# A hybrid encoder layer: stores issued from ScalarE's queue, a convolution of 544 columns, a norm weight applied after the transpose

## The chip, the core and the metric

The kernel runs on one core of a Trainium2 chip. The metric is device microseconds of one launch. The core has TensorE (PE in the profile; its weight loads are PEld), VectorE (DVE), ScalarE (ACT), GpSimd (POOL) and SyncE (SP, which here only issues DMAs). ScalarE and GpSimd can issue DMAs as well; in the profile the part of an engine that issues is called ACTq, POOLq or SPq.

## What is computed

One layer of a streaming encoder, for 1024 new positions of one stream and 64 of another with a cache of 512 positions (T = 1088 columns):

```python
xn = _rmsnorm(x, p['norm_mix_w'])
proj = xn @ p['w_in']
z, xbc, dt_raw, q, k, v, gate_ssm, gate_att = jnp.split(proj, ...)

xbc_c, conv_new = _causal_dwconv(conv_past, xbc, p['ssm_conv_w'], p['ssm_conv_b'])   # width 4
xbc_c = jax.nn.silu(xbc_c)
...
y_ssm, ssm_new = _ssd_scan(xs, dt, a_neg, bm, cm, ssm_past, chunk_len)
y_ssm = _rmsnorm((y_ssm + D * xs) * jax.nn.silu(z), p['ssm_norm_w'])    # by group

q, k = rope(rmsnorm(q)), rope(rmsnorm(k))
o = _diff_attention(q, k_all, v_all, q_pos, k_pos, lam)                 # softmax 1 - lam * softmax 2
o = (_rmsnorm(o, p['subln_w']) * (1.0 - lambda_init)).reshape(b, t, ATT_V_WIDTH)

mix = sigmoid(gate_ssm) * (y_ssm @ p['w_branch_ssm']) + sigmoid(gate_att) * (o @ p['w_branch_attn'])
x = x + mix @ p['w_out']
h = _rmsnorm(x, p['norm_ffn_w']) @ p['w_up']
ha, hb = jnp.split(h, 2, axis=-1)
hc, ffn_new = _causal_dwconv(ffn_past, ha, p['ffn_conv_w'], p['ffn_conv_b'])
x = x + (jax.nn.silu(hc) * hb) @ p['w_down']
```

## The kernel before

Everything is float32. A large product is made of three matmuls on operands split in a high and a low half (`product`, lines 170 to 172: high by high, high by low, low by high). Activations lie transposed, features on partitions and the 1088 columns along the free axis, mostly in four quarters of 272 columns (`CH`).

The stages, with their place in the profiled execution:

- Input projections and the norms of q and k (0 to about 560 us).
- **Attention** (about 560 to 1120 us). `attend` works on one unit, a head and a block of up to 128 rows. Scores go to PSUM (`sc`, lines 1111 and 1112), VectorE takes the maximum (line 1116 or 1120), ScalarE the exponentials (1125), VectorE combines the two softmaxes (1129), PE transposes the result (`pt`, 1140), copies follow, and PE multiplies by the values (`po`, 1160). When a head's nine units are done, `head_out` forms its norm, scales the nine blocks of `o_t` (line 1178), transposes them, splits them in `oh` and `ol`, and stores both to `o_sc`.
- Attention alone would leave PE idle, so **filler** runs among it: `conv_tiles` and `gate_tiles` project the features of the scan and the gates, a quarter of 24 matmuls at a time, into two PSUM banks (`mm`). `conv_tiles` copies each quarter out into `pre` behind three columns of the quarter before (`tail`, copied by GpSimd, line 989), multiplies by the four taps (ScalarE line 999, VectorE three times line 1001), applies SiLU as tanh (ScalarE line 1002, VectorE line 1003), and stores to `x_sc`. `gate_tiles` stores to `g_sc`.
- **The scan** (about 1125 to 1500 us): 36 steps of `front` and `back`, chunk after chunk of 128 columns, four groups; each step loads `bc` with a broadcast from `a_sc`. `gated`, `normed` and `scaled` finish a span of up to 384 columns and store it to `y_sc`. Filler here is the first two branch products: `o` times its weights with the gate, stored to `m_sc`, and half of `y` times its weights, stored to `n_sc`. Side tiles (`b_g`, eight buffers) hold what is loaded beside them and what is stored.
- **The third branch product** (about 1505 to 1610 us) loads the gates (`g_sc`), `n_sc` and `m_sc` through the same side tiles; then output projection and feed-forward part to the end.

Order is not written by hand alone. The program is recorded in the order of the code, with rates that say how much filler goes between units (`ATT_STEPS`, `SCAN_STEPS`), and a scheduler that reckons with its own durations then orders each engine's instructions; `tc.high_priority` and `tc.issue_after` bind it in places. So a lighter instruction can move others. Each engine runs its own queue strictly in order, and a DMA that has to wait for its data holds all that stands behind it in its queue.

Before, every store named above is issued from SP, the queue that also issues nearly all loads (`load` is `nc.sync.dma_start`, `send` is `nc.scalar.dma_start`).

Of the kernel before, what the change touches and what calls it, by code (L numbers as in the profile page):

```python
# [9 lines left out]
F32 = mybir.dt.float32  # L10
R32 = mybir.dt.float32r
AF = mybir.ActivationFunctionType
# [5 lines left out]
P = 128  # L18
D = 1024
# [70 lines left out]
def hybrid_layer(ctx: ExitStack, tc: tile.TileContext, xT, xt, prm, cst, rope, wvd, win, wbs, wba, wout, wup, wdn,  # L90
# [149 lines left out]
                    out(m, c, to)  # L240
                    yield w

    def store(dst):
        return lambda m, c, t: load(out=dst[P * m : P * (m + 1), c : c + t.shape[1]], in_=t)

    def run(gen):
        for _ in gen:
# [729 lines left out]
    def conv_tiles(tiles):  # L977
        for f in tiles:
            tail = None

            def evac(ps, c, w):
                nonlocal tail
                n = min(w, TP - c)
                pre = cv_pool.tile([P, QW + 6], F32, name="pre", tag="pre", bufs=2)
                cc = cv_pool.tile([P, QW + 3], F32, name="cc", tag="cc", bufs=3)
                if tail is None:
                    G.memset(pre[:, 0:3], 0.0)
                else:
                    G.tensor_copy(pre[:, 0:3], tail)  # L989
                S.copy(pre[:, 3 : 3 + n], ps[:, :n])  # L990
                tail, m = pre[:, n : n + 3], w
                if n < w:
                    m = w + 3
                    G.tensor_copy(pre[:, n + 3 : n + 6], par[:, O_CS + 3 * f : O_CS + 3 * f + 3])
                    S.copy(pre[:, n + 6 : w + 6], ps[:, n:])
                    G.tensor_copy(conv_o[:, f, 0:3], tail)
                    G.tensor_copy(conv_o[:, f, 3:6], pre[:, w + 3 : w + 6])
                cw = lambda i: col(O_CW + 4 * f + i)
                act(cc[:, :m], pre[:, :m], AF.Identity, bias=col(O_CB + f), scale=cw(0))  # L999
                for i in range(1, 4):  # L1000
                    V.scalar_tensor_tensor(cc[:, :m], pre[:, i : i + m], cw(i), cc[:, :m], ALU.mult, ALU.add)  # L1001
                seen["tanh"] = act(pre[:, :m], cc[:, :m], AF.Tanh)
                V.scalar_tensor_tensor(cc[:, :m], pre[:, :m], 1.0, cc[:, :m], ALU.add, ALU.mult)  # L1003
                seen["stored"] = load(out=x_sc[P * f : P * (f + 1), c : c + n], in_=cc[:, :n])
                if n < w:
                    load(out=x_sc[P * f : P * (f + 1), c + n : c + w], in_=cc[:, n + 3 : m])

            yield from project(win[B_X + f], evac)

# [23 lines left out]
    with (tc.tile_pool(name="ak", bufs=1) as ak, tc.tile_pool(name="at", bufs=1) as at,  # L1033
          tc.tile_pool(name="psc", bufs=1, space=PSUM) as psc, tc.tile_pool(name="psa", bufs=1, space=PSUM) as pa):
        def head_tiles(h):
            def fetch(name, n, b, parts):
                t = ak.tile([P, n], R32, name=name, tag=name, bufs=b)
                for lo, src in parts:
                    load(out=t[lo : lo + src.shape[0]].bitcast(F32), in_=src)
                return t  # L1040

            by_head = lambda d: [d.rearrange("(x h) t -> h x t", h=16)[2 * h + c] for c in range(2)]
            q, k, ck = by_head(q_st), by_head(k_st), by_head(c_st)
            q_t, kh_t, kl_t, ch_t, cl_t = [[None] * 2 for _ in range(5)]
            sides = ((0, 512), (512, T))
            q_src = lambda c: [(0, q[0])] if c == 0 else [(0, q[1][64:128]), (64, q[1][0:64])]
            twice = lambda src, u: [(0, src[64 * u : 64 * u + 64]), (64, src[64 * u : 64 * u + 64])]

            def component(c, x):
                a, b = sides[x]  # L1050
                for to, name, parts in ((q_t, "q", q_src(c)), (kh_t, "kh", twice(k[c], 0)), (kl_t, "kl", twice(k[c], 1))):
                    to[c] = to[c] or [None] * 2
                    to[c][x] = fetch(f"{name}_{x}", b - a, 3, [(lo, src[:, a:b]) for lo, src in parts])

            def past(u, to, name):
                for c in range(2):
                    to[c] = fetch(name, PAST, 2, twice(ck[c], u))

            v_t = ak.tile([P, 9, P], F32, name="v_t", tag="v_t", bufs=2)
            cv_t = ak.tile([P, 4, P], F32, name="cv_t", tag="cv_t", bufs=2)  # L1060

            def values_of():
                load(out=v_t[:, :8], in_=v[0:TP, P * h : P * (h + 1)].rearrange("(a p) e -> p a e", p=P))
                load(out=v_t[:TS, 8], in_=v[TP:T, P * h : P * (h + 1)])

            def cached():
                past(0, ch_t, "ch_t")
                past(1, cl_t, "cl_t")
                load(out=cv_t, in_=cv[:, P * h : P * (h + 1)].rearrange("(a p) e -> p a e", p=P))

            if h == 0:
                for x in range(2):
                    for c in range(2):
                        component(c, x)
                values_of()
                later.append(cached)
            else:
                for x in range(2):
                    component(0, x)
                values_of()  # L1080
                for x in range(2):
                    component(1, x)
                cached()
            return q_t, kh_t, kl_t, ch_t, cl_t, v_t, cv_t

        def attend(h, i, tiles, o_t, ssq, s0):
# [78 lines left out]
        def head_out(h, o_t, ssq, s0):  # L1165
# [7 lines left out]
            V.tensor_tensor(out=ms, in0=ms, in1=t0, op=ALU.mult)  # L1173
            V.tensor_tensor(out=t1, in0=ms, in1=t0, op=ALU.mult)
            V.scalar_tensor_tensor(rs, t1, 1.5, t0, ALU.add, ALU.mult)
            for i in range(9):
                n = min(P, T - i * P)
                V.scalar_tensor_tensor(o_t[:n, i], o_t[:n, i], rs[:n, i : i + 1], wsub[:n], ALU.mult, ALU.mult)
            yield
            yield  # L1180
            for b0 in range(0, 9, 4):
                pt = pa.tile([P, 512], F32, name="pt2", tag="pt", bufs=2)
                top = min(9, b0 + 4)
                for i in range(b0, top):
                    n = min(P, T - i * P)
                    PE.transpose(pt[:, (i - b0) * P : (i - b0) * P + n], o_t[:n, i], ident[:n, :n])
                w = min(T, top * P) - b0 * P
                hi, lo = (at.tile([P, 512], R32, name=n, tag="a_t", bufs=AT)[:, :w] for n in ("oh", "ol"))
                S.copy(hi, pt[:, :w])
                V.tensor_tensor(out=lo, in0=pt[:, :w], in1=hi, op=ALU.subtract)  # L1190
                for u, t in enumerate((hi, lo)):
                    seen["out"] = load(out=o_sc[D * u + P * h : D * u + P * (h + 1), b0 * P : b0 * P + w], in_=t.bitcast(F32))
                yield

        fill(FIRST)
# [4 lines left out]
        lam = at.tile([P, 4], F32, name="lam")  # L1200
        lt = at.tile([P, 512], F32, name="lt", tag="a_t", bufs=AT)[:, :64]
        wsub = at.tile([P, P], F32, name="wsub")
        V.tensor_scalar_mul(wsub, par[:, O_SUB : O_SUB + P], 1.0 - LAMBDA_INIT)
# [23 lines left out]
        for h in range(8):  # L1227
# [25 lines left out]
    with (tc.tile_pool(name="sin", bufs=1) as sin, tc.tile_pool(name="sp", bufs=1) as sp,  # L1253
# [93 lines left out]
        def scaled(g, c, w, xs, zt, y, rs):  # L1347
# [11 lines left out]
                V.tensor_tensor(out=lo[:, js], in0=y[:, js], in1=hi[:, js], op=ALU.subtract)  # L1359
            for u, t in enumerate((zt, y)):  # L1360
                r0 = D * u + 4 * P * g
                load(out=y_sc[r0 : r0 + 4 * P, c : c + w].rearrange("(j p) t -> p j t", p=P), in_=t)

        ends = []

# [609 lines left out]
```

## Time and profile before

| what | value |
| --- | --- |
| median of three runs | 2420.58 us (2420.09 to 2423.67) |
| the profiled execution | 2425.83 us |
| its span, first to last instruction | 2424.0 us |
| granted TensorE clock | 0.997 |
| busy of the span: PE, PEld, DVE, ACT, POOL | 98%, 95%, 72%, 50%, 30% |
| matmuls | 18648 |

A busy PE is a PE with a matmul under way; the rows of a view give busy time, count and the mean of one instruction, and at the end how long the engine sat idle just before and what ended that. In the views in order of time the first two numbers are the start and the length in us, and a bracket gives the idle time before and its releaser.

### The profile page before, as it was taken

To read this page: it belongs to the slowest core of one execution; us is meant where nothing else is said; L and a number is where in the kernel's file an instruction comes from. 1 tells how busy PE (TensorE), PEld (TensorE's weight loads), DVE (VectorE), ACT (ScalarE), POOL (GpSimd) and SP (SyncE) were. 2 spreads that over 40 slices of the span, in tenths; PEclk is the share of its full clock that TensorE was granted. 3 is DMA by queue.
4 is the path that set the end of the run, shared out by engine and by line. 5 is a ranking of instruction groups with operands and counts; after the bars stand their busy time and mean duration, and the time that the engine had idled before them with its cause. 6 is when DMAs were issued, how large, how long until landed. Compare 5 with 4: busy or idle time off the path is not lost.

```text
span 2424.0 us, 49267 instructions
## 1 busy us (share of the span) xinstructions
PE 2379.3 (98%) x18648; PEld 2306.1 (95%) x18648; DVE 1750.6 (72%) x3150; ACT 1217.8 (50%) x2695; POOL 731.4 (30%) x773
## 2 busy tenths in 40 slices
PE   8999999999999999999999999999999999999998
PEld 8999999999999999999888899999999999999998
DVE  4678987646868778884789776656866767677765
ACT  6454454325656666665666564334543334352442
POOL 0032433321101101111444442012254455444444
PEclk9999999999999999999999999999999999999999
DMA  7773868536555544435978955764124424367976
GB/s 240 274 245 129 265 218 303 168 104 205 163 157 153 164 143 135 143 104 180 352 264 267 344 190 186 210 208 142 66 82 157 143 98 160 127 199 200 245 182 105
DMA packets 295087, 449.78 MB, mean 186 GB/s; under 512 B 36601, under 2 KB 188290, under 8 KB 294850
## 3 DMA queue, kind: packets, MB, share of 16 engines
q1 hardware_dynamic: 265506, 387.00, 49.5%
q0 software_dynamic: 11040, 26.34, 5.5%
q10 hardware_dynamic: 18304, 33.30, 3.7%
q8 instruction: 146, 2.39, 0.4%
q14 instruction: 91, 0.75, 0.1%
HBM read 294.03 MB, written 152.50 MB: 184 GB/s over the span
## 4 chain that ended last, share of the span: by engine, by line
PE 44%; DVE 6%; DMA 3%; issue 2%; ACT 1%; POOL 1%; SPq 0%; POOLq 0%; DVEq 0%; ACTq 0%
PE mx L1617 13%; PE mx L1791 6%; PE mm L1617 5%; PE mm L170 2%; PE mm L172 2%; PE mm L171 2%; PE mx L170 2%; PE mm L1791 2%; PE mx L172 2%; PE mx L171 2%; PE yi L1306 1%; PE stp L1318 1%; PE ye L1312 1%; DMA b<-y_sc 1%; DMA m_sc<-b_g 1%
## 5 line engine op out<-in xcount | busy, mean ns | idle before, releaser
L170 PE MATMUL mm<-b,w_hi 128*128 128x272 f32 x1376 | 408.7, 297 | 0.0
L172 PE MATMUL mm<-b,w_lo 128*128 128x272 f32 x1376 | 404.2, 294 | 0.0
L171 PE MATMUL mm<-b,w_hi 128*128 128x272 f32 x1376 | 403.0, 293 | 0.0
L170 PEld LDWEIGHTS mm<-b,w_hi 128*128 128x128 f32 x1376 | 259.5, 189 | 5.7 <-issue 3.4
L171 PEld LDWEIGHTS mm<-b,w_hi 128*128 128x128 f32 x1376 | 259.6, 189 | 4.5 <-issue 3.1
L172 PEld LDWEIGHTS mm<-b,w_lo 128*128 128x128 f32 x1376 | 259.1, 188 | 3.6 <-issue 2.5
L1617 PE MATMUL mx<-m,w_hi 128*128 128x272 f32 x792 | 152.3, 290 | 1.2 <-ACT m L419 1.2
L420 DVE TENSOR_TENSOR wh<-w_f,wh 128x512 fp32r<-128x512 f32 (+1 forms) x156 | 151.6, 973 | 0.7 <-ACT wh L419 0.7
L1001 DVE SCALAR_TENSOR_TENSOR cc<-pre,par,cc 128x272 f32<-128x272 f32 (+1 forms) x288 | 139.6, 488 | 9.8 <-ACT cc L999 7.5
L1617 PE MATMUL mx<-n,wh 128*128 128x272 f32 x1056 | 141.6, 288 | 1.1 <-DVE u L1644 1.1
L1125 ACT ACTIVATE p_t<-sc,mx 128x512 f32<-128x512 f32 (+6 forms) x144 | 106.2, 740 | 67.5 <-DVE mx L1116 37.4
L1617 PEld LDWEIGHTS mx<-n,wh 128*128 128x128 f32 x1056 | 135.7, 188 | 1.3 <-DVE u L1644 1.3
L989 POOL COPY pre<-pre 128x3 f32<-128x3 f32 x72 | 27.7, 385 | 346.3 <-DVE cc L1003 182.1
L563 POOL TENSOR_TENSOR ws<-w_f 128x512 f32<-128x512 f32 (+1 forms) x51 | 69.3, 1360 | 198.2 <-DMA w_f<-in_win_dram 82.0
L1617 PEld LDWEIGHTS mx<-m,w_hi 128*128 128x128 f32 x792 | 124.4, 188 | 1.4 <-ACT m L419 1.4
L170 PE MATMUL mx<-b,w_hi 128*128 128x272 f32 x416 | 122.9, 296 | 2.0 <-ACT w_hi L155 1.5
L172 PE MATMUL mx<-b,w_lo 128*128 128x272 f32 x416 | 121.5, 294 | 0.0
L171 PE MATMUL mx<-b,w_hi 128*128 128x272 f32 x416 | 121.4, 292 | 0.0
L1617 PE MATMUL mx<-m,w_lo 128*128 128x272 f32 x396 | 114.2, 289 | 0.0
L1626 ACT ACTIVATE cc<-pre,par 128x544 f32<-128x544 f32 (+1 forms) x44 | 37.2, 846 | 146.2 <-DVE pre L1661 145.3
L156 DVE TENSOR_TENSOR w_lo<-w_f,w_hi 128x1024 fp32r<-128x1024 f32 (+1 forms) x74 | 92.8, 1256 | 22.5 <-ACT w_hi L155 22.1
L419 ACT CAST wh<-w_f 128x512 fp32r<-128x512 f32 (+1 forms) x156 | 95.2, 613 | 27.0 <-POOL w_f L569 8.3
(463 smaller groups left out, 7311.7 us busy)
## 6 DMA issues: line engine op xcount, KB each, us to landing
w_f<-in_win_dram SPq DMA_DIRECT2D x40, 512.0 KB, 4.3
w_f<-in_wup_dram SPq DMA_DIRECT2D x80, 256.0 KB, 2.9
w_f<-in_win_dram SPq DMA_DIRECT2D x76, 256.0 KB, 3.3
bc<-a_sc SPq DMA_DIRECT2D x32, 512.0 KB, 7.1
b<-y_sc SPq DMA_DIRECT2D x24, 544.0 KB, 8.1
h_sc<-hb SPq DMA_DIRECT2D x44, 272.0 KB, 2.1
ht<-h_sc SPq DMA_DIRECT2D x22, 544.0 KB, 4.7
t_sc<-ht SPq DMA_DIRECT2D x22, 544.0 KB, 2.9
```

What stands on the lines that cost most here:

```text
L156: V.tensor_tensor(out=lo, in0=w, in1=hi, op=ALU.subtract)
L170: PE.matmul(ps, a_hi, b_hi, start=i == 0, stop=False)
L171: PE.matmul(ps, a_hi, b_lo, start=False, stop=False)
L172: PE.matmul(ps, a_lo, b_hi, start=False, stop=i == n - 1)
L419: S.copy(hi, src)
L420: V.tensor_tensor(out=lo, in0=src, in1=hi, op=ALU.subtract)
L563: G.tensor_tensor(out=s1, in0=q21, in1=q22, op=ALU.add)
L1001: V.scalar_tensor_tensor(cc[:, :m], pre[:, i : i + m], cw(i), cc[:, :m], ALU.mult, ALU.add)
L1125: act(p_t[:n, :nk], sc[c][:n, :nk], AF.Exp, bias=mx[:n, c : c + 1], accum_out=dst)
L1617: PE.matmul(ps, w[x][:, c], b[y][:, k], start=start and k == i == 0, stop=k == 3 and i == 2, skip_group_check=not start)
L1626: act(cc[:, :n], pre[h][:, :n], AF.Identity, bias=col(O_FB + f), scale=cw(0))
L1791: PE.matmul(ps, w[y][:, c], b[z][:, k], start=start and k == j == 0, stop=k == n - 1 and j == 2, skip_group_check=not start)
```

## The change

Four edits, in attention and the scan.

1. Stores of tiles that ScalarE wrote are issued by ScalarE (`send`): `g_sc` in `gate_tiles` (32 stores), the high halves of `o_sc` (24) and `y_sc` (6), and `n_sc` (32). Stores of tiles that VectorE wrote stay on SP, `m_sc` among them.
2. The convolution works on halves of 544 columns. Both quarters are copied into one `pre` tile of 550 columns, and the taps, tanh and store follow once for both. `cc` has two buffers instead of three.
3. In `head_out` the nine scalings by row factor and weight become one multiplication of eight blocks by the row factors, broadcast, and one of the ninth. The weight `wsub`, by column, becomes `wcol`, by partition, through one transpose on PE at the start of attention, and is applied in the two instructions that split the transposed head.
4. The cached keys and values of a head are loaded before its fourth unit instead of at its start, and `cv_t` has one buffer instead of two.

```diff
-    def store(dst):
-        return lambda m, c, t: load(out=dst[P * m : P * (m + 1), c : c + t.shape[1]], in_=t)
+    def store(dst, by):
+        return lambda m, c, t: by(out=dst[P * m : P * (m + 1), c : c + t.shape[1]], in_=t)
...
-                seen["stored"] = load(out=g_sc[P * j : P * (j + 1), c : c + w], in_=gt)
+                seen["stored"] = send(out=g_sc[P * j : P * (j + 1), c : c + w], in_=gt)
...
             def evac(ps, c, w):
-                nonlocal tail
+                nonlocal tail, pre
+                first = c % HT == 0
+                if first:
+                    pre = cv_pool.tile([P, HT + 6], F32, name="pre", tag="pre", bufs=2)
+                    if tail is None:
+                        G.memset(pre[:, 0:3], 0.0)
+                    else:
+                        G.tensor_copy(pre[:, 0:3], tail)
+                at = 3 + c % HT
                 n = min(w, TP - c)
-                pre = cv_pool.tile([P, QW + 6], F32, name="pre", tag="pre", bufs=2)
-                cc = cv_pool.tile([P, QW + 3], F32, name="cc", tag="cc", bufs=3)
...
-                S.copy(pre[:, 3 : 3 + n], ps[:, :n])
+                S.copy(pre[:, at : at + n], ps[:, :n])
                 if n < w:
...
+                if first:
+                    return
+                c -= QW
+                n, m = min(HT, TP - c), HT
+                tail = pre[:, n : n + 3]
...
+                cc = cv_pool.tile([P, HT + 3], F32, name="cc", tag="cc", bufs=2)
                 act(cc[:, :m], pre[:, :m], AF.Identity, bias=col(O_CB + f), scale=cw(0))
...
-            cv_t = ak.tile([P, 4, P], F32, name="cv_t", tag="cv_t", bufs=2)
+            cv_t = ak.tile([P, 4, P], F32, name="cv_t", tag="cv_t")
...
-            for i in range(9):
-                n = min(P, T - i * P)
-                V.scalar_tensor_tensor(o_t[:n, i], o_t[:n, i], rs[:n, i : i + 1], wsub[:n], ALU.mult, ALU.mult)
+            V.tensor_tensor(out=o_t[:, :8], in0=o_t[:, :8], in1=rs[:, :8].unsqueeze(2).to_broadcast([P, 8, P]), op=ALU.mult)
+            V.tensor_scalar(o_t[:TS, 8], o_t[:TS, 8], rs[:TS, 8:9], None, ALU.mult)
...
-                S.copy(hi, pt[:, :w])
-                V.tensor_tensor(out=lo, in0=pt[:, :w], in1=hi, op=ALU.subtract)
+                act(hi, pt[:, :w], AF.Copy, scale=wcol)
+                V.scalar_tensor_tensor(lo, pt[:, :w], wcol, hi, ALU.mult, ALU.subtract)
                 for u, t in enumerate((hi, lo)):
-                    seen["out"] = load(out=o_sc[...], in_=t.bitcast(F32))
+                    seen["out"] = (send, load)[u](out=o_sc[...], in_=t.bitcast(F32))
...
+        pw = pa.tile([P, 512], F32, name="pw", tag="pt", bufs=2)
+        PE.transpose(pw[:, :P], wsub, ident)
+        S.copy(wcol, pw[:, 0:1])
...
+                if x == 3 and later:
+                    later.pop()()
...
-                load(out=y_sc[r0 : r0 + 4 * P, c : c + w].rearrange("(j p) t -> p j t", p=P), in_=t)
+                (send, load)[u](out=y_sc[r0 : r0 + 4 * P, c : c + w].rearrange("(j p) t -> p j t", p=P), in_=t)
...
-            yield from branch(True, side, o_sc, wba, D, (), store(m_sc))
-            yield from branch(True, side, y_sc[: 2 * D], wbs[0], None, (), store(n_sc))
+            yield from branch(True, side, o_sc, wba, D, (), store(m_sc, load))
+            yield from branch(True, side, y_sc[: 2 * D], wbs[0], None, (), store(n_sc, send))
```

PE executes the same matmuls in both kernels, and one transpose more after the change. How the instructions move is shown at three places.

SP, from the last spans of the scan (`y_sc<-y`) to the first loads of the third branch product (line 200), before:

```order
L218 DMA b_19331<-y_sc 128x4x272
L244 DMA n_sc<-b_g 128x272
L1353 DMA y_sc<-y 128x4x320
L218 DMA b_19339<-y_sc 128x4x272
L244 DMA n_sc<-b_g 128x272
L154 DMA w_f<-in_wbs_dram 128x1024
L218 DMA b_19341<-y_sc 128x4x272
L218 DMA b_19351<-y_sc 128x4x272
L244 DMA n_sc<-b_g 128x272 x3
L200 DMA b_g<-g_sc 128x272
L200 DMA b_g<-n_sc 128x272
```

The same place after the change (line 1365 is the `y_sc` store):

```order
L218 DMA b_18799<-y_sc 128x4x272
L1365 DMA y_sc<-y 128x4x320
L218 DMA b_18807<-y_sc 128x4x272
L154 DMA w_f<-in_wbs_dram 128x1024
L218 DMA b_18809<-y_sc 128x4x272
L218 DMA b_18819<-y_sc 128x4x272
L200 DMA b_g<-g_sc 128x272
L200 DMA b_g<-n_sc 128x272
```

The five `n_sc` stores (line 244) are gone from here; they stand in ScalarE's queue, each behind the copy that fills its tile.

VectorE, at the start of head 2's second unit, the wide one of rows 896 to 1023 (`ors` are the row factors of head 1, `sc` and `mx` scores and maxima of head 2's units), before:

```order
L1115 MEMSET sc 64x64
L1003 SCALAR_TENSOR_TENSOR cc<-pre,cc 128x272
L1169 TENSOR_TENSOR ms<-ms,ssq 128x9
L1116 TENSOR_REDUCE mx<-sc 128x1
L1236 MEMSET ssq 128x9
L1172 TENSOR_SCALAR ms<-ms 128x9
L1173 TENSOR_TENSOR ms<-ms,on_9065 128x9
L1174 TENSOR_TENSOR on_9066<-ms,on_9065 128x9
L1175 SCALAR_TENSOR_TENSOR ors<-on_9066,on_9065 128x9
L1178 SCALAR_TENSOR_TENSOR o_t<-o_t,ors,wsub 128x128 x4
L1127 RECIPROCAL sm<-sm 128x1
L1178 SCALAR_TENSOR_TENSOR o_t<-o_t,ors,wsub 128x128 x4
```

After the change, where line 1136 is the combination of the unit's softmaxes and lines 1183 and 1184 are the scaling:

```order
L1135 SCALAR_TENSOR_TENSOR sm<-sm,nlam,s_8796 128x1
L1127 TENSOR_REDUCE mx<-sc 128x2
L1136 SCALAR_TENSOR_TENSOR p_t<-p_t,sm 128x1024
L1180 TENSOR_TENSOR ms<-ms,on_8921 128x9
L1009 SCALAR_TENSOR_TENSOR cc<-pre,par,cc 128x544
L1134 RECIPROCAL sm<-sm 128x1
L1181 TENSOR_TENSOR on_8922<-ms,on_8921 128x9
L1009 SCALAR_TENSOR_TENSOR cc<-pre,par,cc 128x544
L1135 SCALAR_TENSOR_TENSOR sm<-sm,nlam,s_8796 128x1
L1182 SCALAR_TENSOR_TENSOR ors<-on_8922,on_8921 128x9
L1183 TENSOR_TENSOR o_t<-o_t,ors 128x1024
L1184 TENSOR_SCALAR o_t<-o_t,ors 64x128
```

The scaling of the finished head has moved behind the wide unit's combination (`p_t` 128x1024); before, it stood ahead of it. On PE, between this unit's last score and its first transpose, stood 72 filler matmuls before and stand 54 after the change.

VectorE again, near the end of attention, where head 6's scaling meets the maxima of a wide unit of head 7, before:

```order
L1115 MEMSET sc 64x64
L1178 SCALAR_TENSOR_TENSOR o_t<-o_t,ors,wsub 128x128 x8
L1178 SCALAR_TENSOR_TENSOR o_t<-o_t,ors,wsub 64x128
L1001 SCALAR_TENSOR_TENSOR cc<-pre,par,cc 128x272
L1116 TENSOR_REDUCE mx<-sc 128x1
```

And after the change:

```order
L1183 TENSOR_TENSOR o_t<-o_t,ors 128x1024
L1184 TENSOR_SCALAR o_t<-o_t,ors 64x128
L1122 MEMSET sc 64x64
L1011 SCALAR_TENSOR_TENSOR cc<-pre,cc 128x544
L1122 MEMSET sc 64x64
L1123 TENSOR_REDUCE mx<-sc 128x1 x2
```

The scaling keeps its place ahead of the maxima; nine instructions have become two.

More of the change, by code (lines that the diff above doesn't have):

```diff
@@ L1004, in evac @@
                 seen["stored"] = load(out=x_sc[P * f : P * (f + 1), c : c + n], in_=cc[:, :n])
-                if n < w:
-                    load(out=x_sc[P * f : P * (f + 1), c + n : c + w], in_=cc[:, n + 3 : m])
+                if n < HT:
+                    load(out=x_sc[P * f : P * (f + 1), c + n : c + HT], in_=cc[:, n + 3 : m])
             yield from project(win[B_X + f], evac)
@@ L1082, in head_tiles @@
                     component(1, x)
-                cached()
+            later.append(cached)
             return q_t, kh_t, kl_t, ch_t, cl_t, v_t, cv_t
@@ L1188, in head_out @@
                 hi, lo = (at.tile([P, 512], R32, name=n, tag="a_t", bufs=AT)[:, :w] for n in ("oh", "ol"))
-                S.copy(hi, pt[:, :w])
-                V.tensor_tensor(out=lo, in0=pt[:, :w], in1=hi, op=ALU.subtract)
+                act(hi, pt[:, :w], AF.Copy, scale=wcol)
+                V.scalar_tensor_tensor(lo, pt[:, :w], wcol, hi, ALU.mult, ALU.subtract)
                 for u, t in enumerate((hi, lo)):
-                    seen["out"] = load(out=o_sc[D * u + P * h : D * u + P * (h + 1), b0 * P : b0 * P + w], in_=t.bitcast(F32))
+                    seen["out"] = (send, load)[u](out=o_sc[D * u + P * h : D * u + P * (h + 1), b0 * P : b0 * P + w], in_=t.bitcast(F32))
                 yield
@@ L1202, in hybrid_layer @@
         wsub = at.tile([P, P], F32, name="wsub")
+        wcol = at.tile([P, 1], F32, name="wcol")
         V.tensor_scalar_mul(wsub, par[:, O_SUB : O_SUB + P], 1.0 - LAMBDA_INIT)
+        pw = pa.tile([P, 512], F32, name="pw", tag="pt", bufs=2)
+        PE.transpose(pw[:, :P], wsub, ident)
+        S.copy(wcol, pw[:, 0:1])
         for i in range(2):
```

17 lines of the change are left out of this document (6 added, 11 removed).

## The prediction

> **What bounds the kernel now.** I read the page's head first, then the busy time by stretch, then the waits of TensorE alone. Only TensorE is nearly always busy, and the change touches two stretches: attention (540 to 1100 us) and the scan with the branch products (1100 to 1560).
>
> ```profile
> span 2424.0 us, 49267 instructions
> PE 2379.3 (98%) x18648; PEld 2306.1 (95%) x18648; DVE 1750.6 (72%) x3150; ACT 1217.8 (50%) x2695; POOL 731.4 (30%) x773
> ...
> 540.00:1100.00 560.00, 557.24 (x4274) 535.05 (x4274) 441.95 (x1062) 355.36 (x954) 67.39 (x164) 1.00 0.49 150
> 1100.00:1560.00 460.00, 449.60 (x3606) 410.09 (x3606) 337.35 (x464) 263.82 (x619) 163.56 (x108) 1.00 0.78 255
> ```
>
> The columns are length, then busy time with instruction counts for PE, PEld, DVE, ACT, POOL, then the granted clock, DMA share and GB/s. PE is idle for 560 - 557.24 = 2.76 us in attention and for 460 - 449.60 = 10.40 us after it. The clock is full. So 13.2 us is all that lighter side engines can give back: 0.5% of the time. What those microseconds wait for is in the view of waits, for PE from 540 to 1560 us:
>
> ```profile
> PE yi L1306 <- DVE y L1314: 3.1, 2, 1.6
> PE tr L1285 <- DVE xx L1294: 2.3, 3, 1.4
> PE mx L170 <- ACT w_hi L155: 1.5, 1, 1.5
> PE sc L1111 <- ACT p_t L1125: 1.1, 1, 1.1
> PE stp L1318 <- DVE state L1325: 1.0, 2, 0.8
> ...
> PE yi L1306 <- ACT y L1316: 0.7, 1, 0.7
> PE cb L1287 <- ACT b_cb L1290: 0.6, 1, 0.6
> ...
> PE gst L1340 <- POOL zin L1336: 0.5, 1, 0.5
> ```
>
> Total us, times and longest stand behind each. The six rows on yi, tr, stp, cb and gst are the scan's: 3.1 + 2.3 + 1.0 + 0.7 + 0.6 + 0.5 = 8.2 us. The row of sc is attention's, the row of w_hi belongs to the branch products behind the scan.
>
> **The wider convolution and the norm.** Their prices, before and in the nearest rows of the new shape:
>
> ```profile
> L1001 DVE SCALAR_TENSOR_TENSOR cc<-pre,par,cc 128x272 f32<-128x272 f32 (+1 forms) x288 | 139.6, 488 | 9.8 <-ACT cc L999 7.5
> L1003 DVE SCALAR_TENSOR_TENSOR cc<-pre,cc 128x272 f32<-128x272 f32 x94 | 40.6, 432 | 6.8 <-ACT pre L1002 6.5
> L1628 DVE SCALAR_TENSOR_TENSOR cc<-pre,par,cc x88: 773/786/1884, 1729.8 to 2188.9; 128x544 f32<-128x544 f32 x44, 128x546 f32<-128x546 f32 x44
> L1178 DVE SCALAR_TENSOR_TENSOR o_t<-o_t,ors,wsub x72: 332/343/373, 651.9 to 1126.2; 128x128 f32<-128x128 f32 x64, 64x128 f32<-64x128 f32 x8
> L156 DVE TENSOR_TENSOR w_lo<-w_f,w_hi 128x1024 fp32r<-128x1024 f32 x29 | 35.3, 1216 | 2.5 <-ACT w_hi L155 2.4
> ```
>
> VectorE's convolution falls from 288 x 0.488 + 96 x 0.432 = 182 us to 144 x 0.786 + 48 x 0.73 (an estimate: 0.786 less the 0.056 that separates the first two rows) = 148 us, so 34 us less. The norm's 72 x 0.343 = 24.7 us become 8 x (1.216 + at most 0.343) = 12.5 us, 12 us less. ScalarE's two passes and GpSimd's copies halve in number as well. None of these 46 us is on the path by itself: VectorE has 560 - 442 = 118 us idle in attention. They count where PE waits for VectorE, and that is one place, shown in order of time:
>
> ```profile
> 1061.41 2.47 DVE L1178 SCALAR_TENSOR_TENSOR o_t<-o_t,ors,wsub 128x128 f32<-128x128 f32 x9
> ...
> 1064.22 1.07 DVE L1116 TENSOR_REDUCE mx<-sc 128x1 f32<-128x896 f32 x1
> 1065.33 1.01 ACT L1125 ACTIVATE p_t<-sc,mx 128x896 f32<-128x896 f32 x1 [2.63 <-DVE mx L1116]
> 1066.48 0.39 PE L1111 MATMUL sc<-kh,q 128*128 128x256 f32 x1 [1.08 <-ACT p_t L1125]
> ```
>
> The nine scalings of a finished head (2.47 us) hold back the maximum, that holds back the exponential, and PE waits 1.08 us for the score banks. In the new order the scaling still stands ahead of these maxima, but takes about 1.2 + 0.3 us. That is 1.0 us sooner, less 0.2 to 0.3 because the convolution instruction between them grows from 0.43 to 0.73 us. Term: **-0.8 us** (bounds -1.1 and 0).
>
> The added transpose `pw` is one more instruction on PE ahead of the first scores. Its nearest row is the transposes of attention:
>
> ```profile
> L1140 PE MATMUL pt<-con,p_t x328: 221/272/331, 584.4 to 1116.6; 128*128 128x128 f32 x144, 64*128 64x64 f32 x16, 64*64 64x64 f32 x4
> ```
>
> Term: **+0.3 us** (0 to 0.6, if it also waits a little for `wsub`). Carrying `wcol` as a scale costs no instruction.
>
> **The tighter order.** The scheduler reckons with the lighter VectorE and brings transposes closer behind their scores. The tightest case is unit 7 of head 2. Its last score and the end of its softmax were:
>
> ```profile
> 714.06 0.39 PE L1112 MATMUL sc<-kl,q 128*128 128x512 f32 x1
> ...
> 724.68 1.27 DVE L1129 SCALAR_TENSOR_TENSOR p_t<-p_t,sm 128x1024 f32<-128x1024 f32 x1
> ...
> 1061.89 0.29 PE L172 MATMUL mm<-b,w_lo 128*128 128x272 f32 x1
> 1063.78 0.29 PE L172 MATMUL mm<-b,w_lo 128*128 128x272 f32 x1
> ```
>
> So 725.95 - 714.45 = 11.5 us of softmax. The last two rows give the pace of filler: 15 matmuls from one to the other, 0.126 us each. The new order leaves 54 filler matmuls and about 1.9 us of attention's own between the two, where 72 stood: 54 x 0.126 + 1.9 = 8.7 us. If the softmax stayed as long, PE would wait 11.5 - 8.7 = 2.8 us. But nine scalings (9 x 0.343 = 3.1 us) no longer stand inside it. Bounds 0 and +2.8; I take **+1.0 us**, nearer the lower one. The single `cv_t` buffer waits for nothing: its load is now issued at the fourth unit and read by the ninth.
>
> **Stores from ScalarE.** 32 of `g_sc`, 24 of `o_sc`, 6 of `y_sc` and 32 of `n_sc`, 94 in all, leave SP. What one costs ScalarE when work follows directly:
>
> ```profile
> 349.58 0.33 ACTq L681 DMA_DIRECT2D z_sc<-pre  x1
> 349.95 0.39 ACT L688 COPY u<-mx 128x272 f32<-128x272 f32 x1 [0.40 <-ACT pre L666]
> ```
>
> That is 0.33 to 0.40 us, 31 to 38 us over 94, on an engine idle for 205 us in attention and for 196 after it: nothing on the path where it is covered, and the rival below where it is not. What it gives shows at two places on SP. First, in the scan:
>
> ```profile
> 1273.36 0.37 SPq L1362 DMA_DIRECT2D y_sc<-zin  x1
> ...
> 1280.07 5.58 DMA m_sc<-b_g
> 1285.67 0.32 SPq L200
> 1286.04 3.92 DMA bc<-a_sc
> ...
> 1291.89 0.33 PE L1306 MATMUL yi<-bc,xx 128*64 128x128 f32 x2 [1.64 <-DVE y L1314]
> ```
>
> The middle rows are from the chain that ended last. A store of `m_sc` lands after 5.58 us, SP waits for it before it reuses a side tile, the load of `bc` stands behind that on SP, and PE waits 1.64 us soon after. The big `y_sc` store of the same queue was issued just ahead. With the six of them on the other queue I expect `m_sc` to land sooner, and half of the scan's 8.2 us to go: **-4.1 us** (bounds -8.2 and, since the order changes too, +1.6, one more wait like the longest of them). That half is a choice: the waits on yi, whose chain this is, are 3.8 of the 8.2.
>
> The Trainium skill's page "DMA: Bandwidth & Descriptors" (Issuing engines are not separate DMA queues) speaks against this: DMAs of all issuing engines share the same 16 DMA engines and interleave, and spreading them saves only issue time on the sequencer. By that the term would be nothing and the sum -1.0 us, the first rival below; the trace of before does not decide it.
>
> Second, where the scan ends and the third branch product begins:
>
> ```profile
> 1506.33 1.95 SPq L244 DMA_DIRECT2D n_sc<-b_g  x3
> 1508.33 0.62 SPq L200 DMA_DIRECT2D b_g<-g_sc  x1
> ...
> 1513.35 3.86 DMA b_g<-n_sc
> ...
> 1528.34 0.43 ACT L226 ACTIVATE b_g<-b_g 128x272 f32<-128x272 f32 x1 [0.89 <-DMA b_g<-n_sc]
> 1528.68 1.03 ACT L155 CAST w_hi<-w_f 128x1024 fp32r<-128x1024 f32 x1
> ```
>
> The third row is from the chain, the others from the timeline. Three `n_sc` stores take SP 1.95 us right ahead of the branch's first loads; the chain of those loads, the tanh and the casts runs until ScalarE reaches the weight cast at 1528.68, for which PE waits 1.5 us. The new order has no store there, so the loads can start 2 us sooner: **-1.5 us** (bounds -1.5 and 0).
>
> **The sum.** -0.8 + 0.3 + 1.0 - 4.1 - 1.5 = -5.1 us. The profiled execution took 2425.83 us, of which 2424.0 are span; it would take 2420.7. It is 5.2 us above the median of the runs, 2420.58, so the forecast for the median is 2415.5 us, 0.21% less.
>
> **Rivals.**
> - *The stores bring only issue time.* The scan's 8.2 us stay; the other terms hold: -0.8 + 0.3 + 1.0 - 1.5 = -1.0 us, 2419.6. For it: `m_sc` remains on SP, with the loads that VectorE needs behind it, and VectorE itself is busy 337 of 460 us there. Against it: the 5.58 us landing right behind a large store. Chance 0.37.
> - *ScalarE's stores hold up the banks* (slower). Each makes ScalarE wait for its own result before the next copy out of PSUM. In scan and branch 38 of them stand, between exponentials and copies on which PE depends; at 0.40 us that is 15.2 us. If half reaches PE: +7.6 - 1.0 = +6.6 us, 2427.2. It decides once 15 of the 38 delay PE, since 15 x 0.40 = 6.0 exceeds the gain of 1.0 and the bound of 4.8 together. Against it: ScalarE is idle 43% of that stretch, and has issued such stores all through the input stage. Chance 0.13.
> - *The order falls worse throughout*: waits of the kind of 2.8 us above at several units and in the scan, +5 us or more, about 2426. Chance 0.08.
>
> **How the numbers follow.** The forecast has the remaining chance, 0.42. A change within 0.2% (4.8 us) is about what a measurement of this kernel cannot tell from none; the three runs lie 3.6 us apart. Faster by more than that is the forecast, 0.42; the first rival lies within, 0.37; the other two are slower, 0.21. The range begins at 2409, where nearly all 13.2 us of idle time would be gone, and ends at 2428, just past the case in which half the stores reach PE.
>
> **What would show it.** Right: PE idle from 1100 to 1560 near 5 us instead of 10.40; no wait of PE on `w_hi` near 1528; none of 1 us on `p_t`; VectorE 46 us less busy; `bc` loads with shorter waits of SP on `m_sc`. Wrong: the same waits on yi and tr in the scan (first rival); new waits of PE on copies by ScalarE, with ScalarE idle behind its own stores (second); waits on `p_t` before transposes around unit 7 of head 2 (third).

## The result and the profile after

The changed kernel is slower: 2432.64 us median (2427.73 to 2435.62, six runs) against 2421.47 (2420.09 to 2424.81, six runs). The ratio is 1.0042, 95% interval 1.0028 to 1.0055. The forecast was 2415.5 us, and the range 2409 to 2428 misses the median by 4.6 us. The profiled execution of the changed kernel took 2427.73 us, the shortest of its runs, so this trace shows less than the whole loss: its span is only 2.0 us longer than before's.

The page's head and the busy time by stretch, after (columns as in the prediction):

```profile
span 2426.0 us, 48596 instructions
PE 2380.8 (98%) x18649; PEld 2308.7 (95%) x18649; DVE 1712.4 (71%) x2902; ACT 1202.7 (50%) x2600; POOL 704.6 (29%) x725
...
540.00:1100.00 560.00, 558.65 (x4295) 537.68 (x4295) 416.96 (x826) 339.73 (x864) 40.29 (x118) 1.00 0.48 150
1100.00:1560.00 460.00, 445.47 (x3536) 405.90 (x3535) 328.63 (x441) 261.98 (x610) 165.63 (x106) 0.99 0.77 253
```

VectorE is 38 us less busy. In attention PE's idle time fell from 2.76 to 1.35 us. From 1100 to 1560 us it rose from 10.40 to 14.53 us, and the granted clock, 1.00 before, is 0.99. The waits of PE in that stretch, after:

```profile
PE tr L1297 <- DVE xx L1306: 3.0, 2, 2.4
PE yi L1318 <- ACT y L1328: 2.5, 1, 2.5
PE cb L1299 <- ACT b_cb L1302: 1.8, 1, 1.8
PE yi L1318 <- DVE bc L1310: 1.4, 2, 1.2
PE gst L1352 <- POOL zin L1348: 1.4, 1, 1.4
PE yi L1318 <- DVE y L1326: 0.8, 2, 0.5
...
PE mx L170 <- ACT w_hi L155: 0.4, 1, 0.4
```

The lines stand 12 higher than before's (L1318 is L1306's matmul). The longest wait was 1.64 us before; now three are of 2.4 us, 2.5 us and 1.8 us, and two of them are on ScalarE. The row that the prediction wanted shorter, yi on VectorE's `y`, did fall, from 3.1 to 0.8 us; other rows took its place.

**The wait of 2.5 us** is told by the chain of waits from 1139 to 1152 us (start, us, what), and by ScalarE's row in order of time:

```profile
1140.93 7.37 DMA w_f<-in_wba_dram
...
1148.33 0.02 ACTq L973
...
1148.38 0.33 ACTq L973
1148.71 0.04 issue
1148.75 0.59 ACT y L1328
1149.34 0.04 issue
1149.39 1.09 PE yi L1318 x16
```

```profile
1145.30 2.45 ACT L1309 ACTIVATE bc<-bc,nacum 128x128 f32<-128x128 f32 x8
1148.38 0.33 ACTq L973 DMA_DIRECT2D g_sc<-gt  x1
1148.75 0.59 ACT L1328 COPY y<-yi 128x512 f32<-128x512 f32 x1 [1.00 <-DMA w_f<-in_wba_dram]
```

ACTq L973 is a store of `g_sc` from ScalarE's queue. It has nothing to do with the weights `w_f`, yet it waited until they had landed, and ScalarE's copy of `y` out of PSUM stood behind it, and PE behind that. By the trace's semaphore records SP's and ScalarE's transfers take eight semaphores in turn, and this store has the semaphore of the eighth transfer before it, that load. But ScalarE was busy with exponentials until 1147.75 us, so the store accounts for 1.0 us of the 2.5 (the bracket of the copy: 0.6 us for the landing, the rest for the issue). The rest is the exponentials ahead of it, 0.8 us, and the copy itself, 0.6 us. At 1366 us the same happens with an `n_sc` store. There ScalarE had been idle since 1363.3 us, and the whole wait of 1.8 us is the store's:

```profile
1357.54 8.96 DMA m_sc<-b_g
1366.50 0.02 issue
1366.52 0.02 ACTq L244
1366.54 0.04 issue
1366.58 0.34 ACTq L244
1366.92 0.04 issue
1366.96 0.38 ACT b_cb L1302
```

So these two stores account for 2.8 us of the 14.53 us of idle time.

**After some waits PE runs at half speed.** Five stretches of the changed kernel in the view of busy time, the granted clock third from the end; the first is the wait of 2.5 us itself, at full clock; the stretch from 1188 us stands behind two waits of 1.2 and 0.5 us:

```profile
1146.50:1149.30 2.80, 0.41 (x4) 0.18 (x2) 0.00 (x0) 1.80 (x7) 0.00 (x0) 1.00 1.08 354
1150.40:1153.80 3.40, 3.40 (x16) 3.24 (x15) 2.97 (x5) 2.19 (x8) 2.10 (x2) 0.50 1.04 370
1153.80:1158.00 4.20, 4.20 (x38) 3.37 (x37) 3.17 (x5) 1.43 (x6) 0.76 (x1) 1.00 1.08 386
1188.00:1194.80 6.80, 6.24 (x28) 5.32 (x27) 6.80 (x9) 3.70 (x11) 2.46 (x2) 0.50 1.00 345
1379.10:1382.50 3.40, 3.14 (x15) 3.04 (x16) 3.40 (x6) 1.64 (x7) 1.40 (x1) 0.50 0.49 187
```

PE was busy 3.40 + 6.24 + 3.14 us at half speed, which costs half of that, 6.4 us. Before has no such stretch in the scan. So the scan costs 4.1 us of idle time and 6.4 us of clock more, 10.5 together, and the rest of the span gives 8.5 back. Much of that is attention. These are the scores' and the products' rows of before, then of after; the first and last starts are what counts:

```profile
L1111 PE MATMUL sc<-kh,q x208: 191/341/500, 566.0 to 1095.7; 128*128 128x512 f32 x73, 128*128 128x384 f32 x8, 128*128 128x256 f32 x8, 128*64 128x64 f32 x8
L1160 PE MATMUL po<-v_t,a_t x592: 269/275/377, 589.0 to 1120.1; 128*128 128x128 f32 x192, 64*64 64x128 f32 x6
```

```profile
L1118 PE MATMUL sc<-kh,q x208: 191/341/497, 564.8 to 1091.5; 128*128 128x512 f32 x73, 128*128 128x384 f32 x8, 128*128 128x256 f32 x8, 128*64 128x64 f32 x8
L1167 PE MATMUL po<-v_t,a_t x592: 269/275/356, 587.0 to 1115.1; 128*128 128x128 f32 x192, 64*64 64x128 f32 x6
```

From the first score to the last product: 554.1 us before, 550.3 after. About 0.9 us of the 3.8 is filler that the new order puts into the scan.

### The profile page after: what moved, and what is told of

Its sections match the earlier page's. It is cut to its first block, busy times and chain, and to the rows that moved or that the text cites. A ratio compares the mean times of both kernels' runs of the same rounds, so it can differ in the third digit from the quotient of the medians.

```text
span 2426.0 us, 48596 instructions
## 1 busy us (share of the span) xinstructions
PE 2380.8 (98%) x18649; PEld 2308.7 (95%) x18649; DVE 1712.4 (71%) x2902; ACT 1202.7 (50%) x2600; POOL 704.6 (29%) x725
## 4 chain that ended last, share of the span: by engine, by line
PE 54%; DVE 5%; DMA 4%; issue 2%; ACT 1%; POOL 1%; SPq 0%; ACTq 0%; POOLq 0%; DVEq 0%
PE mx L1629 13%; PE mx L1803 6%; PE mm L1629 5%; PE mm L170 4%; PE mm L172 4%; PE mm L171 4%; PE mx L170 2%; PE mx L172 2%; PE mx L171 2%; PE mm L1803 2%; PE po L1167 2%; PE yi L1318 1%; PE ye L1324 1%; DMA b<-y_sc 1%; PE sc L1119 1%
## 5 line engine op out<-in xcount | busy, mean ns | idle before, releaser
L1009 DVE SCALAR_TENSOR_TENSOR cc<-pre,par,cc 128x544 f32<-128x544 f32 (+1 forms) x144 | 111.3, 773 | 8.7 <-ACT cc L1007 7.4
L1646 POOL TENSOR_TENSOR hb<-hb,cc 128x544 f32<-128x544 f32 (+2 forms) x63 | 66.8, 1074 | 136.8 <-DVE hb L1667 102.1
```

Of the source, the lines that this page charges most:

```text
L1646: (V if f + 1 == FT else G).tensor_tensor(out=hb[h][:, o : o + n], in0=hb[h][:, o : o + n], in1=cc[:, d : d + n], op=ALU.mult)
```

## The experiments

Four theories stand against each other. **T1**: a store in ScalarE's stream waits for a landing and holds up the copies behind it. **T2**: any edit makes the scheduler order the scan anew, and the order of before has few waits. **T3**: the wide convolution. **T4**, seen in the traces of the first runs: VectorE's `bc` product meets GpSimd's gate product and takes several times as long. PE's idle time is that from 1100 to 1560 us throughout. Unless said otherwise an interval is of the ratio to before.

**e1: no moved stores; e2: moved stores alone; e3: wide convolution and late load alone; e4: transposed norm weight alone.**

```diff
-seen["stored"] = send(out=g_sc[...]      # e1; also o_sc, y_sc and store(n_sc, send)
+seen["stored"] = load(out=g_sc[...]
```

> The changed kernel with all its stores back on SP's queue; the wide convolution and the transposed weight stay. Before 2421.5 us, after 2432.6 us, PE waits between 1100 and 1560 us 10.4 and 14.5 us. Theory T1 (stores in ScalarE's stream hold up its exponentials and copies in the scan): the loss goes, 2419 to 2422 us, PE waits there 10 us or less. T2 (the program's order of the scan's matmuls, drawn anew by any edit, leaves the chain of tr, VectorE and yi less room at some steps): this order is a third one, different from both, so the time may stand anywhere from 2418 to 2435 us, and it goes with the PE waits from 1100 to 1560 us. T3 (the wide convolution: it is gone from 1100 us on only if it ends in time, and its VectorE pieces are twice as long): 2430 to 2434 us.

> The kernel before with the stores of g_sc, o_sc (high half), y_sc (high half) and n_sc from ScalarE's queue, and nothing else. PE's order is unlike that of before over some 4000 matmuls from the middle of attention to the scan's end. T1: 2428 to 2433 us, all of the loss, with PE waits on copies and exponentials of ScalarE. T2: not the stores decide but where the scan's steps stand; an order nearer to that of before than the others, so 2418 to 2426 us. T3: 2416 to 2422 us. The prediction's own terms would give 2420.6 - 4.1 - 1.5 = 2415 us.

> The kernel before with the convolution of 544 columns and the later load of the cached values alone. T1: as before, 2419 to 2423 us. T2: a new order again, 2418 to 2435 us, by the PE waits from 1100 to 1560 us. T3: 2430 to 2434 us, all of the loss, with waits of matmuls for PSUM banks that the convolution's copies free late, or of yi for VectorE behind a 544-wide piece.

> The kernel before with the norm's weight applied after the transpose alone. T1: 2420 us (the -0.8 and +0.3 us of the prediction). T3: the same. T2: a new order here as well, 2418 to 2435 us, and where it stands away from 2420 us the difference lies in PE waits from 1100 to 1560 us, in which the norm has no instruction.

Measured: e1 1.0035 (1.0023 to 1.0047), e2 1.0047 (1.0035 to 1.0059), e3 1.0052 (1.0037 to 1.0066), e4 1.0000 (0.9992 to 1.0009). Stores alone cost what the whole change costs, and so does the convolution alone; both together cost no more. T1 and T3 each explain one of these runs and fail at another. T2's own number for e2, 2418 to 2426 us, missed too (2434.4). The idle times are 17.7, 19.8, 19.4 and 10.2 us. In e3, without a moved store, PE waits twice near 1300 us. The first wait, 3.89 us, is for a load of `in`. The second, 3.06 us, shows T4 (VectorE, then GpSimd, then PE; start, us, instruction, wait before it):

```profile
1293.08 7.59 DVE L1307 TENSOR_TENSOR bc<-bc,b_cb 64x512 f32<-64x512 f32 x1 [2.56 <-ACT bc L1306]
1300.60 0.67 DVE L1323 TENSOR_TENSOR y<-y,yi 128x512 f32<-128x512 f32 x1
```

```profile
1290.91 3.44 POOL L1342 TENSOR_TENSOR y<-y,zin 128x1536 f32<-128x1536 f32 x1
1294.31 1.04 POOL L1332 TENSOR_TENSOR state<-state,decs 128x512 f32<-128x512 f32 x1
...
1296.37 1.81 POOL L1344 TENSOR_TENSOR zin<-zin 128x768 f32<-128x768 f32 x1
```

```profile
1296.81 1.09 PE L1294 MATMUL tr<-con,in 128*128 128x128 f32 x4 [3.89 <-DMA in<-x_sc]
...
1301.42 0.91 PE L1315 MATMUL yi<-bc,xx 128*64 128x128 f32 x6 [3.06 <-DVE y L1323]
```

A product whose shortest time is 0.67 us took 7.59 while GpSimd worked through its queue. The next row, of the same kernel, shows the half clock behind the two waits:

```profile
1301.50:1313.00 11.50, 11.50 (x58) 8.34 (x58) 5.73 (x9) 5.43 (x13) 1.22 (x2) 0.50 0.55 180
```

**e9: scan's stores alone; e10: attention's stores alone; e11: only `g_sc`; e12: only `o_sc`**, each on the kernel before.

```diff
-seen["stored"] = load(out=g_sc[...]      # e11; e12 the o_sc line, e10 both, e9 y_sc and n_sc
+seen["stored"] = send(out=g_sc[...]
```

> The kernel before with only the scan's stores (y_sc high half, n_sc) from ScalarE's queue. PE's order keeps that of before up to PE instruction 8735, in the scan, and moves little behind it. T1 (ScalarE's stores themselves): nearly all of e2's loss, 2431 to 2435 us. T2 (where the scan's steps stand in PE's order): near to before, 2419 to 2427 us, and again the span is 2413.5 us plus PE's idle time from 1100 to 1560 us, as in the six profiles so far (2411.5 to 2414.8).

> The kernel before with only the stores of g_sc and o_sc (high half) from ScalarE's queue. None of these is waited for by the scan's chain from tr to yi; but PE's order changes from the middle of attention to the scan's end as it does with all four stores. T1: as before, 2420 to 2424 us. T2: as e2, 2428 to 2436 us, with the waits in the scan.

> The kernel before with only the stores of g_sc, 32 pieces of gate, from ScalarE's queue. Attention's o_sc stores stay on SP's queue. T1 in the form 'a store in ScalarE's stream that waits for another transfer's landing holds up the copies behind it': the 17 of these stores that lie in the scan carry e10's loss, 2430 to 2435 us. T2 (PE's order of the scan): the order changes here from PE instruction 6183 on, 2378 lines of it, less than e10's 3056; 2422 to 2435 us.

> The kernel before with only the high halves of o_sc stored from ScalarE's queue, all but the last head's three stores before 1100 us. PE's order changes only between PE instructions 6584 and 8793, in attention and the scan's first steps, and is that of before from there on. T1: no store of ScalarE in the scan, so 2420 to 2424 us. T2: most of the scan's order is that of before, so 2419 to 2426 us.

Measured: e9 1.0010 (1.0001 to 1.0019), e10 1.0048 (1.0033 to 1.0062), e11 1.0030 (1.0017 to 1.0044), e12 1.0006 (0.9995 to 1.0017). The 38 stores inside the scan, which rival 2 had priced, cost 0.1% where PE's order is that of before up to 1203 us (e9, idle 10.6 us). The `g_sc` stores cost 0.3%, with an order that differs from the middle of attention on. T2's ranges hold all four (e12 at the edge); T1's miss e9 and e10 and hold e11 at the edge. In e11's trace the last `g_sc` store that held ScalarE up stands at 1171.6 us, and two waits of PE lie beside such stores, 1.4 and 0.5 us. Of the 6.3 us of idle time that e11 has more than before, 2.9 us lie behind 1200 us, and so does its 1.7 us of half clock; ScalarE has no such store there.

**How much of the order changed.** Of the 3604 matmuls that PE runs from 1100 to 1560 us in before, so many have another one in their place, counted in the traces: 1738 in the changed kernel; 1569 in e1, 1625 in e3, 1722 in e4; 1147, 1143 and 1135 in e2, e10 and e11; 784 in e9, 80 in e12. Two things follow. First, a new order need not cost anything: e4's differs as much as the changed kernel's and loses nothing. Second, e2, e10 and e11 have almost one order (e2 differs from e10 in 28 places of all 18648, e11 in 131). They are one sample of T2, not three, and all store `g_sc` from ScalarE, so no run parts the two there.

**Neutral shifts of the order: the filler's rate in the scan, on the kernel before and on the changed one.** The work, the queues and the instructions stay the same.

```diff
-SCAN_STEPS = 1.17
+SCAN_STEPS = 1.16      # b_ss116, a_ss116; 1.18 in b_ss118, a_ss118
```

> The kernel before with the filler's rate in the scan at 1.16 steps instead of 1.17: the same work, the same queues, the same instructions; one step of filler in some hundred comes later, and PE's order changes only from instruction 9448 on. T1 and T3: as before, 2419 to 2424 us. T2: the order of before is a lucky or chosen one, so a neutral shift costs as an edit does: anywhere from 2418 to 2435 us, and by PE's idle time from 1100 to 1560 us.

> The changed kernel with the same shift of the filler's rate, 1.16 instead of 1.17: all parts of the change stay. T1 and T3: as after, 2430 to 2435 us, since stores and convolution are as they were. T2: another order, 2416 to 2435 us; a time under 2424 us would show that the loss is in the order and not in the parts of the change.

> The kernel before with the filler's rate in the scan at 1.18 instead of 1.17, the other way from the run at 1.16 (2427.5 us): a second neutral shift of the order. T1 and T3: 2420 to 2424 us. T2: like the shift to 1.16, a few us slower than the order that 1.17 gives, 2421 to 2435 us.

> The changed kernel with the filler's rate at 1.18 instead of 1.17. At 1.17 it took 2432.6 us, at 1.16 2442.0. T1 and T3: 2430 to 2435 us. T2: anywhere from 2416 to 2445 us, with the span at 2411 to 2417 us plus PE's idle time from 1100 to 1560 us; below 2420 us it would be a version that beats both kernels.

Measured: on before 1.0023 (1.0013 to 1.0032) and 0.9996 (0.9987 to 1.0005); on the changed kernel 1.0079 (1.0067 to 1.0091) and 1.0055 (1.0041 to 1.0069). The order alone moves the time by 5 us on the one and 9 us on the other (2442.0 us in a_ss116, above every forecast), but in these four it does not close the gap between them.

**f1 to f4: the gate product on VectorE**, which takes T4's longest partner off GpSimd: in the changed kernel without moved stores (f1), in the changed kernel (f2), in before (f3), in the changed kernel with the scan's stores back (f4).

```diff
-            G.tensor_tensor(out=y, in0=y, in1=zt, op=ALU.mult)
+            V.tensor_tensor(out=y, in0=y, in1=zt, op=ALU.mult)
```

> The changed kernel without its moved stores (as e1, 2432.3 us), and the scan's gate product (y by z, 128x1536, 12 of them) on VectorE instead of GpSimd, where one took 3.46 us. T4 (VectorE's bc product, 1.2 us alone, took up to 7.6 us where it met that product on GpSimd): the 13 us that VectorE loses there beyond before's go, and PE's idle time from 1100 to 1560 us falls from 17.7 to about 10 us: 2420 to 2425 us, in spite of some 12 x 1.6 = 19 us more of work on VectorE. T2: still anywhere from 2420 to 2440 us, most likely slower, since VectorE has more to do.

> The changed kernel, all of it, with the gate product on VectorE. T4 says little here: VectorE's excess beside GpSimd was 22.8 us, less than before's 25.5, so its time stays near 2430 us or falls by 2 to 5 us. T1: the waits behind ScalarE's stores stay (2.5 us at 1149, 1.8 us at 1367): 2427 to 2433 us. T2: 2420 to 2440 us.

> The kernel before with the gate product on VectorE: the control. T4: before has an excess of 25 us beside GpSimd and only 10.4 us of PE idle time from 1100 to 1560 us, so a small gain or none: 2416 to 2422 us. T2: a new order, 2420 to 2435 us.

> As f2, with the scan's own stores (y_sc, n_sc) back on SP's queue; the stores of g_sc and o_sc stay on ScalarE's. T1: against f2 the waits of PE for copies held up by n_sc and y_sc stores at 1350 to 1400 us go, 3 to 4 us: 2424 to 2429 us. T2: 2420 to 2440 us with no place told ahead. If f1 and f4 both come under 2421 us, the attention half of the change is worth keeping with this product moved.

Measured: f1 1.0019 (1.0010 to 1.0028), f2 1.0033 (1.0020 to 1.0046), f3 1.0006 (0.9995 to 1.0016), f4 1.0039 (1.0027 to 1.0051). In f1 VectorE's 36 `bc` products took 47.1 us instead of e1's 70.3, and the longest fell from 7.6 to 2.4 us. The time fell by 4 us (the intervals of e1 and f1 overlap), not by the 8 to 12 expected. The idle time did not fall at all, as the rows of e1 and f1 show: other waits took its place. Of the 5.1 us by which f1's span is shorter, 2.6 are half clock in the scan.

```profile
1100.00:1560.00 460.00, 442.34 (x3524) 403.00 (x3523) 342.20 (x439) 260.99 (x608) 159.81 (x106) 0.98 0.78 252
```

```profile
1100.00:1560.00 460.00, 442.32 (x3525) 401.80 (x3524) 336.20 (x455) 259.84 (x607) 122.89 (x94) 0.99 0.77 253
```

So T4 is a real price in e1 and e3, but not the cause of the loss. f4 against f2 shows no gain from the scan's stores going back, and f1, which has none of the moved stores, stands 0.14% below f2, with intervals that overlap: T1 alone isn't it either.

**A shift of the filler's rate in attention**, which orders everything from there on anew.

```diff
-ATT_STEPS = 1.12
+ATT_STEPS = 1.11
```

> The kernel before with the filler's rate in attention at 1.11 instead of 1.12: the same work, queues and instructions; PE's order changes from instruction 5392, in attention, to the end of the scan. PE's idle time from 1100 to 1300 us was 3.9 us in before, 10.6 with g_sc stored by ScalarE, 16.2 with the wide convolution, 7.3 in the changed kernel. T2 (the order alone): it may come out anywhere between, 4 to 16 us, and the time at 2421 to 2435 us, most likely slower than before. Theory of the parts: without the parts it stays at 4 to 5 us, and the time at 2419 to 2425 us.

> The changed kernel with the same shift in attention. T2: a new draw from attention on, 2418 to 2440 us, idle 1100 to 1300 us 4 to 16 us. Theory of the parts: 2430 to 2436 us, with 7 us or more of idle time there and the wait behind a g_sc store near 1149 us in it.

Measured: b_at111 1.0055 (1.0043 to 1.0068), a_at111 1.0029 (1.0017 to 1.0041). The kernel before, with no part of the change and the same work, loses as much as the whole change does. Its row:

```profile
1100.00:1560.00 460.00, 441.01 (x3486) 400.78 (x3486) 330.47 (x441) 258.93 (x605) 164.34 (x108) 0.99 0.76 249
```

19.0 us of idle time, and four stretches of half clock in the scan. The changed kernel loses rather less by the same shift than without it (1.0029 against 1.0042, the intervals overlap). The time, 2436.6 us, is just above T2's range. T2 allows for a loss in the kernel before; no other theory does.

**All 20 traces together.** For each, the span less PE's idle time from 1100 to 1560 us, less half of PE's busy time in stretches of half clock there:

| kernels | scan's idle time and clock loss, us | rest of the span, us |
|---|---|---|
| before | 10.4 | 2413.6 |
| ten others with the narrow convolution | 10.2 to 25.8 | 2408.8 to 2415.7 |
| after | 20.9 | 2405.0 |
| eight others with the wide convolution | 20.2 to 33.7 | 2404.2 to 2408.7 |

Each figure is from one execution, and the executions of one kernel lie up to 12 us apart (before: 2417.3 to 2429.0 us on one chip). The rows also mix orders with edits. Between them, the wide convolution, always together with the late load, goes with 5.7 us less outside the scan (means 2406.3 and 2412.0), and all nine kernels that have it lose 20 us or more in the scan.

**What stays open** is the cause of the changed kernel's own loss. Shown is that the same work in another order can lose as much (b_at111); that this is what the change did is argued, since no shift of the changed kernel brought it back to before. Open too is why none of the nine stands lower. Either it is again the order, of which nine is a small sample that starts alike, or what attention gains is given back at once. For the second speaks the scan's start, shown here for before and then after:

```profile
1140.00:1160.00 20.00, 20.00 (x176) 18.09 (x175) 13.00 (x15) 16.19 (x47) 7.24 (x6) 1.00 1.02 346
1160.00:1180.00 20.00, 20.00 (x161) 17.65 (x160) 11.47 (x17) 11.96 (x28) 13.47 (x9) 1.00 1.09 375
1180.00:1200.00 20.00, 19.36 (x143) 15.80 (x143) 19.21 (x22) 14.77 (x40) 10.62 (x7) 1.00 1.10 367
```

```profile
1140.00:1160.00 20.00, 17.43 (x140) 15.25 (x139) 11.79 (x14) 12.44 (x37) 5.63 (x6) 0.91 1.07 370
1160.00:1180.00 20.00, 20.00 (x168) 17.36 (x167) 15.15 (x20) 14.89 (x39) 14.55 (x10) 1.00 1.08 358
1180.00:1200.00 20.00, 16.69 (x106) 14.13 (x104) 19.64 (x19) 11.65 (x29) 15.18 (x6) 0.83 0.93 314
```

In both the DMA engines are full (share 1.0 and more, 0.93 in the last row) and VectorE is nearly full from 1180 to 1200 us (19.2 and 19.6 of 20). A kernel that arrives earlier finds the same two. This was not tried by itself. No run beats both kernels: b_ss118 (0.9996), e4 (1.0000), e12 and f3 (both 1.0006) cannot be told from before.

## Why the prediction was wrong

- **The step that failed is the scan's term, -4.1 us** ("`m_sc` to land sooner, and half of the scan's 8.2 us to go"). Its first link did not hold: with the big `y_sc` stores on the other queue, `m_sc` stores landed after a median of 5.2 us instead of 4.9. The scan got 4.1 us more of idle time instead of 4.1 less, plus 6.4 us of half clock that no term had. Here is the landing of before, then of after, from the view of `m_sc` between 1200 and 1520 us (shortest, median, longest):

```profile
DMA to landing us min/median/max: 1.8/4.9/10.0
```

```profile
DMA to landing us min/median/max: 1.8/5.2/10.6
```

  The rule of the Trainium skill that the prediction set against this term (page "DMA: Bandwidth & Descriptors", section Issuing engines are not separate DMA queues: the transfers of all issuing engines share the same 16 engines) was right here: nothing landed sooner. The pairs that differ in the moved stores agree: 4.9 in before and 4.8 in e2, 5.4 in e1 and 5.2 in after.
- **The bounds of that term were the second fault.** They gave a new order +1.6 us, "one more wait like the longest of them". Neutral shifts moved the time by up to 13 us. Rival 3 is nearest to what the runs show, with a chance of 0.08 and a price of +5, but for the scan alone: in attention the waits fell. Its mechanism, that the scan's few waits in before belong to one order and not to the stage, belonged in the bounds of every term.
- **Rival 2 had the place and not the mechanism.** It priced the issue of a store at 0.40 us and counted 38 stores in scan and branch; eleven `g_sc` stores issue there too, behind 1125 us. What held PE up was mostly the wait for another transfer's landing: 1.0 us, issue included, and 1.8 us at two stores. In e9, where the 38 alone moved, PE's idle time rose by 0.2 us.
- **Attention's norm, -0.8 us**: the wait on `p_t` at 1066 us fell from 1.1 to two of at most 0.5; e4, with this part alone, is 1.0000. At the transpose `pw` PE waited 0.5 us, by the view for a load of `q`; +0.3 was forecast. **The tighter order, +1.0**, did not show: no wait of PE before a transpose stands in attention's view. The 54 filler matmuls were there, but the softmax of that unit took 7.2 us instead of 11.5.
- **The wide convolution was taken for hidden**, its 34 us of VectorE's time worth nothing. Attention became about 3 us shorter with it, and over all traces the rest outside the scan 5.7 us. The term was missed in the kernel's favour.
- **The third branch, -1.5 us**, came out at -1.1 (the wait on `w_hi` is 0.4 us), but not by its reason: in e1 and e4, with the `n_sc` stores on SP, it is 0.6 and 0.5 us as well.

## What to carry to other kernels

Where a scheduler orders a stage anew after each edit, first find how far a neutral edit moves the time, and judge the parts against that spread: here it is 0.5%, as much as the dearest part showed alone. Trust a part only over several orders, and set the bounds of each term by them. Count also how many orders were really drawn: three edits can give almost the same one. A store moved to a compute engine's queue stalls that engine not only for its issue but until an earlier, unrelated transfer has landed, if the two share a semaphore; look for that in the chain of waits before putting stores between copies that TensorE waits for.

## What the runs showed of the hardware

- Half clock comes in pieces of 3.4 us or a multiple, behind waits of 2.5 us (after, at 1150), of 1.5 us (e11, at 1301.5), and of 1.2 and 0.5 us together (after, at 1188); but not behind each: f4 has a wait of 3.0 us at 1149 and none. What the 20 traces show is a grid of 3.41 us that the half-clock stretches of one execution keep. From 1100 to 1560 us every window of that grid with more than 1.9 us of idle time is followed by half clock, of those with 1.0 to 1.9 us only some, and f4's wait lies across two windows, 1.2 and 1.8 us. The Trainium skill's page "TensorE: Matmul & The Clock Gate" (What's actually happening) has a free-running window of 3413 ns and a fall to half rate after an idle window. The length agrees; the waits here are shorter than one window.
- VectorE's two-input product stood for 7.59 us while GpSimd ran several products in a row. The Trainium skill's page "SBUF — State Buffer" (SBUF: two separate sides) says that a VectorE operation with two SBUF inputs and a GpSimd operation that reads SBUF exclude each other for a whole instruction. The trace agrees, and shows in addition that VectorE did not get in between two of GpSimd's.
